# Softmax division by a diagonal product, a projection's input in quarters, and a later residual load in a hybrid attention and DeltaNet layer

## The chip, the cores and the metric

The kernel runs on one core of a Trainium2 chip. The metric is the device time of one execution in microseconds (us), taken as the median of three runs. Inside the core, TensorE (PE) multiplies matrices, VectorE (DVE), ScalarE (ACT) and GpSimd (POOL) work element by element, and the queues of SyncE (SP) and ScalarE issue transfers. TensorE has a granted clock, given in profiles as a share of 2.4 GHz; 0.50 is its lower level, 1.2 GHz.

## The reference

One layer of a decoder over 1024 positions of width 1024, all in float32. Two groups of heads read one projection of the normalized input, and their outputs are put side by side and projected back.

```
u = rmsnorm(h, norm_mix);  proj = u @ w_in          # 1024 x 2824
aq, ak, av, dq, dk, dv, dz, db, da = split(proj)
# group A: 8 query heads, 2 key heads of 64, blocks of 128 queries, each sees its own and the previous block
s = where(valid, q.k * scale, -inf)
probs = softmax(concat([s, sink]))[..., :-1];  o = probs @ v
# group B: gated DeltaNet, 4 heads of 128, chunks of 64: convolution, SiLU, an inverse per chunk, a scan over 16 chunks
h += concat([attn_out, dn_out]) @ w_o
h += square(relu(rmsnorm(h) @ w_up)) @ w_down
h += sigmoid(rmsnorm(h) @ w_ple_gate) * (p @ w_ple_proj)     # p: 1024 x 256, w_ple_proj: 256 x 1024
out = rmsnorm(h, norm_final)
```

The softmax divides each row of exponentials by its sum (with the sink in it).

## The kernel before

The positions are worked in two halves of 512 (hb = 0 and 1). Large products run in three passes: `split` (L218) writes the rounded part of a float32 tile with ACT and the remainder with POOL or DVE, and PE adds high x high, high x low and low x high. `wunit2` (L277) loads one piece of a weight (128x512) through SP, and splits it.

The order of the work is made when the program is built. Functions are written as generators. An object `flow` keeps a clock of its own: `Pe` (L93 to L107) adds an assumed duration for each product and transposition, `yield 2.5` means "not before 2.5 us from now", and at each step the first task whose time has come is asked for its next piece. If none is due, a piece of `flow.filler` is taken, which is the list of large projections in `projections` (L1085); if that is held up, a piece of `flow.spare`. A float32 product of 128 columns counts twice what a transposition counts in this clock. So a task with more assumed work lets fewer pieces of the filler in between, and they come later.

Four places matter here.

- Attention. `attention` (L585) goes through 32 units of 128 queries and two heads. `att_scores` (L532) makes the scores, the masked maximum (DVE), the exponentials and their sum (ACT), the reciprocal and the division (DVE, L558, on tile `s`). Three units later `att_pt` (L561) transposes the divided probabilities on PE, by products with the identity `con` (through L106), into a PSUM bank from the ring "d", copies them to `pt`, and `att_pv` multiplies by the values.
- `embed` (L1049) computes p @ w_ple_proj as the spare work. It loads p by halves (`pr`, L1055) and splits each half into AT0, of which there is one buffer: the second half's split waits until all products of the first half are done. For each of 4 column groups there are 4 blocks of positions, each pair of blocks a bank: 12 products, an ACT copy into `po` (two buffers, L1072), and a store to `PD` in HBM by SP (L1075).
- `w_out` (L1004) multiplies the concatenated heads by w_o and adds the residual x, which an ACT queue loads by two blocks of 1 MB at the start (L1006, into tiles H and AT).
- The scan of group B: a chain of small steps on PE, DVE and ACT per chunk (products with `St`, `vn`, `oS`), for hb = 0 beside `embed`, for hb = 1 beside `w_out`. The last scan steps of hb = 1 use oss, Z and oS.

After them come the two MLP products and the rest, which the change doesn't touch.

Of the kernel before, what the change touches and what calls it, by code (L numbers as in the profile page):

```python
# [10 lines left out]
F32 = mybir.dt.float32  # L11
F32R = mybir.dt.float32r
AF = mybir.ActivationFunctionType
ALU = mybir.AluOpType
# [4 lines left out]
P = 128  # L19
# [4 lines left out]
HB = 512  # L24
# [7 lines left out]
WN = 2 * NKV  # L32
# [77 lines left out]
def bc(ap, dim, n):  # L110

    a = ap.unsqueeze(dim)
    shape = list(a.shape)
    shape[dim] = n
    return a.to_broadcast(shape)
# [3 lines left out]
def hybrid_block(ctx, tc, t, out):  # L119
    nc = tc.nc  # L120
    V, A, G, SY = nc.vector, nc.scalar, nc.gpsimd, nc.sync
    flow = Flow()
    T = Pe(tc, flow)
    cnt = [0]

    def nm(s):
        cnt[0] += 1
        return f"{s}{cnt[0]}"
# [6 lines left out]
    wraw = pool("wraw", bufs=2)  # L135
# [39 lines left out]
    def part(tag, dt=F32):  # L175

        return keep.tile([P, 2048], dt, tag=tag, name=nm(tag))
# [6 lines left out]
    ident = con[:, K_ID:K_ID + P]  # L184
# [33 lines left out]
    def split(hi, lo, src, lo_eng):  # L218
        A.copy(hi, src)  # L219
        lo_eng.tensor_tensor(lo, src, hi.bitcast(F32), op=ALU.subtract)  # L220
# [227 lines left out]
    atp = atx.__enter__()  # L448
# [84 lines left out]
    def att_scores(n, gp, kv, qT):  # L533

        lo = 0 if n else P
        h0 = kv * 4 + gp * 2
        st = lambda x: atp.tile([P, 2], F32, tag=x, name=nm(x), bufs=4)
        b, free = yield from take("d")
        mx, sm = st("mx"), st("sm")
        s = atp.tile([P, 2, 257], F32, tag="s", name=nm("s"), bufs=4)  # L540
        G.tensor_copy(s[:, :, 256], sinkB[:, h0:h0 + 2])
        b = b.rearrange("p (g s) -> p g s", g=2)
        j = slice(n % 4 + lo // P, n % 4 + 2)
        for i in range(2):
            o = b[:, i, lo:256].rearrange("p (j s) -> p j s", s=P)
            T.matmul(o, qT[:, kv, gp * 2 + i], kH[:, kv, j], start=True, stop=False)
            T.matmul(o, qT[:, kv, gp * 2 + i], kL[:, kv, j], start=False, stop=True)
        for i in range(2):
            V.tensor_tensor_reduce(
                out=s[:, i, lo:256], in0=b[:, i, lo:256], in1=amask[:, lo:256],  # L550
                scale=1.0, scalar=NEG, op0=ALU.add, op1=ALU.max, accum_out=mx[:, i:i + 1])
        free()
        V.scalar_tensor_tensor(mx, mx, -1.0, nsink[:, h0:h0 + 2], op0=ALU.mult, op1=ALU.min)  # L553
        for i in range(2):
            A.activation(s[:, i, lo:257], s[:, i, lo:257], AF.Exp, bias=mx[:, i:i + 1],  # L555
                         accum_out=sm[:, i:i + 1])
        V.reciprocal(sm, sm)
        V.tensor_tensor(s[:, :, lo:256], s[:, :, lo:256], bc(sm, 2, 256 - lo), op=ALU.mult)  # L558
        return s

    def att_pt(n, kv, s):  # L561
        b, free = yield from take("d")
        b = b.rearrange("p (k g s) -> p k g s", k=2, g=2)
        kbs = slice(0 if n else 1, 2)
        for kb in range(kbs.start, 2):
            for i in range(2):
                T.transpose(b[:, kb, i], s[:, i, kb * P:(kb + 1) * P], ident)
        pt = atp.tile([P, 2, 2, P], F32, tag="pt", name=nm("pt"), bufs=2)
        (A.copy if kv else V.tensor_copy)(pt[:, kbs], b[:, kbs])
        free()  # L570
        return pt
# [12 lines left out]
    def attention(ns):  # L584
        units = [(n, gp, kv) for n in ns for gp in range(2) for kv in range(2)]  # L585
        qT, ss, pts, b = {}, {}, {}, None
        lag = 3
        qT[ns[0]] = yield from att_q(ns[0])
        yield 3.0
        for i in range(len(units) + lag):  # L590
            if i < len(units):
                n, gp, kv = units[i]
                ss[i] = yield from att_scores(n, gp, kv, qT[n])
                scored[n].done = gp * kv == 1
                if i + 1 < len(units) and units[i + 1][0] not in qT:
                    qT[n + 1] = yield from att_q(n + 1)
            if i >= lag:
                n, gp, kv = units[i - lag]
                pts[kv] = yield from att_pt(n, kv, ss.pop(i - lag))
                if not kv:  # L600
                    yield 2.5
                    continue
                yield 2.0
                if gp == 0:
                    b, free = yield from take("d")
                att_pv(n, gp, pts, b)
                if gp:
                    free()
                yield 1.76
            else:  # L610
                yield 1.08
# [387 lines left out]
    def hT(hb, j, n=1):  # L999

        x, o = (H, XW + j * HB) if hb == 0 else (H, j * HB) if j < 4 else (AT[1], (j - 4) * HB)
        return x[:, o:o + n * HB]

    def w_out(hb):  # L1004
        for j in (0, 4):
            A.dma_start(hT(hb, j, 4).rearrange("p (j s) -> p j s", j=4),  # L1006
                        t["xT"].rearrange("(j p) s -> p j s", p=P)[:, j:j + 4, hb * HB:hb * HB + HB])

        def rhs(b, kt):
            return dn1[b][:, kt - 4] if hb and kt > 3 else uview(R1, b, kt)  # L1010

        def steps(g, bs, ks):
            for kt in ks:
                if kt % 2 == 0:
                    w = wunit2(t["w_o"], kt // 2, g * 256, (G, G)[hb])
                for m in range(2):
                    o = kt % 2 * 256 + m * P
                    (mm3h, mm3h)[hb](bs[m][0], lambda a: w[:, a, o:o + P], lambda b: rhs(b, kt), kt == 0, kt == KT - 1)
                    if kt < KT - 1 or m == 0:
                        yield  # L1020
            if kt == KT - 1:
                for m in range(2):
                    h = hT(hb, g * 2 + m)
                    V.tensor_tensor(h, bs[m][0], h, op=ALU.add)
                    bs[m][1]()
                yield

        early = ["gg", "ge", "ee"] if hb else []
        held = []
        for g, names in enumerate(early):  # L1030
            if "e" in names:
                yield prepped
            bs = []
            for k in names:
                bs.append((yield from take(k)))
            yield from steps(g, bs, range(4))
            held.append(bs)
        if hb:
            yield pairs_done[1]
        for g in range(4):  # L1040
            if g < len(held):
                yield from steps(g, held[g], range(4, KT))
                continue
            bs = []
            for k in "gg":
                bs.append((yield from take(k)))
            yield from steps(g, bs, range(KT))

    def embed():  # L1049

        for hb in range(2):
            pT = part("AT0", F32R).rearrange("p (b k s) -> p b k s", b=2, k=2)
            for kt in range(2):
                raw = wraw.tile([P, WN], F32, tag="raw", name=nm("pr"))[:, :HB]
                SY.dma_start(raw, t["pT"][kt * P:(kt + 1) * P, hb * HB:(hb + 1) * HB])  # L1055
                split(pT[:, 0, kt], pT[:, 1, kt], raw, G)
            for g in range(4):
                w = wunit2(t["w_proj"], 0, g * 256, G)
                for m in range(0, 4, 2):
                    ring["g"].n -= 1  # L1060
                    b = bank(ps["g"])
                    for kt in range(2):
                        for i in range(2):
                            for j, (x, y) in enumerate(PASSES):
                                T.matmul(b[:, i * 256:i * 256 + 256],
                                         pT[:, x, kt, (m + i) * P:(m + i + 1) * P],
                                         w[:, y, kt * 256:kt * 256 + 256],
                                         start=kt + i + j == 0, stop=kt * i == 1 and j == 2)
                            if kt + i < 2:
                                yield  # L1070
                    o = cvp.tile([P, HB], F32, tag="cv", name=nm("po"))
                    A.copy(o, b)  # L1072
                    ring["g"].n += 1
                    r = hb * HB + m * P
                    SY.dma_start(PD[r:r + 2 * P, g * 256:g * 256 + 256].rearrange("(i p) c -> p i c", p=P),  # L1075
                                 o.rearrange("p (i c) -> p i c", i=2))
                    yield
# [52 lines left out]
    b = bank(ps["e"])  # L1130
# [351 lines left out]
    for kt in range(KT):  # L1482
        for nh in range(2):
            i = kt * 2 + nh
# [11 lines left out]
    for tt in range(NT):  # L1496
# [8 lines left out]
        for q in range(2):  # L1505
            b = bank2()
# [99 lines left out]
```

## Time and profile before

| | us |
|---|---|
| median of three runs | 1365.46 (1364.79 to 1365.91) |
| the profiled execution | 1366.2 |
| its span | 1364.1 |
| PE busy in the span | 1317.7 (97%) |
| DVE busy | 838.8 (61%) |
| ACT busy | 548.0 (40%) |
| POOL busy | 434.5 (32%) |

The profiled execution is 2.1 us longer than its span. In that execution attention runs from about 80 to 290 us, the embedding product between about 390 and 450, w_out from 445 to 565, and the MLP after 565. The rows below carry all numbers of the prediction. A row with a start shows when a run of like instructions began, how long it took until its last one ended, and in square brackets what the engine waited for ahead of it.

### The profile page before, as it was taken

To read this page: it belongs to the slowest core of one execution; us is meant where nothing else is said; L and a number is where in the kernel's file an instruction comes from. 1 tells how busy PE (TensorE), PEld (TensorE's weight loads), DVE (VectorE), ACT (ScalarE), POOL (GpSimd) and SP (SyncE) were. 2 spreads that over 40 slices of the span, in tenths; PEclk is the share of its full clock that TensorE was granted. 3 is DMA by queue.
4 is the path that set the end of the run, shared out by engine and by line. 5 is a ranking of instruction groups with operands and counts; after the bars stand their busy time and mean duration, and the time that the engine had idled before them with its cause. 6 is when DMAs were issued, how large, how long until landed. Compare 5 with 4: busy or idle time off the path is not lost.

```text
span 1364.1 us, 20392 instructions
## 1 busy us (share of the span) xinstructions
PE 1317.7 (97%) x7664; PEld 1125.5 (83%) x7664; DVE 838.8 (61%) x1558; ACT 548.0 (40%) x1083; POOL 434.5 (32%) x430
## 2 busy tenths in 40 slices
PE   8999999999998999898999999999999999999997
PEld 6788688999897998886788888877888888888886
DVE  6786977697564755797776676654333343344553
ACT  6456375544544433564333333342122231221333
POOL 6673626631385452300011111103122212210332
PEclk9999999999999999999999999999999999999999
DMA  6322222324135431321433323354333333232211
GB/s 223 88 54 73 54 62 52 74 73 105 34 119 176 133 110 33 115 85 63 146 116 116 124 87 114 109 185 136 96 116 101 98 123 120 77 93 73 75 62 47
DMA packets 102738, 134.33 MB, mean 98 GB/s; under 512 B 16400, under 2 KB 71744, under 8 KB 102384
## 3 DMA queue, kind: packets, MB, share of 16 engines
q1 hardware_dynamic: 90528, 110.50, 27.0%
q10 hardware_dynamic: 11760, 21.77, 4.4%
q8 instruction: 60, 0.98, 0.3%
q0 software_dynamic: 352, 0.76, 0.2%
q14 instruction: 38, 0.31, 0.1%
HBM read 106.77 MB, written 26.23 MB: 98 GB/s over the span
## 4 chain that ended last, share of the span: by engine, by line
PE 74%; DVE 11%; DMA 6%; ACT 3%; issue 3%; POOL 2%; SPq 1%; POOLq 0%; ACTq 0%; DVEq 0%
PE bk L102 72%; PE bk L106 2%; DVE w L220 1%; DVE cv L412 1%; DMA AD<-t 1%; ACT w L219 1%; DMA raw<-in_w_in 1%; POOL rsb L358 1%; DMA PD<-po 1%; DMA raw<-in_w_down 1%; DMA H<-in_w_in 1%; DMA AT<-in_xT 0%; DVE gg L649 0%; DMA raw<-AD 0%; SPq L841 0%
## 5 line engine op out<-in xcount | busy, mean ns | idle before, releaser
L102 PE MATMUL bk<-T,w 128*128 128x512 f32 x2304 | 537.9, 392 | 5.7 <-ACT w L219 4.5
L102 PEld LDWEIGHTS bk<-T,w 128*128 128x128 f32 x2304 | 432.8, 188 | 102.6 <-ACT w L219 6.6
L220 POOL TENSOR_TENSOR w<-raw,w 128x512 fp32r<-128x512 f32 x136 | 180.5, 1329 | 621.3 <-ACT w L219 590.2
L219 ACT CAST w<-raw 128x512 fp32r<-128x512 f32 (+1 forms) x280 | 172.6, 620 | 460.8 <-PE bk L102 340.6
L102 PE MATMUL bk<-R,w 128*128 128x256 f32 (+1 forms) x1536 | 240.7, 312 | 1.4 <-ACT w L219 1.4
L102 PEld LDWEIGHTS bk<-R,w 128*128 128x128 f32 x1536 | 210.8, 189 | 22.9 <-issue 2.3
L220 DVE TENSOR_TENSOR w<-raw,w 128x512 fp32r<-128x512 f32 (+1 forms) x144 | 107.5, 748 | 61.1 <-ACT w L219 60.9
L1478 DVE TENSOR_TENSOR H<-bk,H 128x512 f32<-128x512 f32 x96 | 64.6, 690 | 96.0 <-PE bk L102 96.0
L102 PE MATMUL bk<-U,w 128*128 128x512 f32 (+1 forms) x384 | 80.3, 355 | 1.0 <-ACT ba L472 0.6
L102 PEld LDWEIGHTS bk<-U,w 128*128 128x128 f32 x384 | 60.2, 191 | 14.5 <-issue 4.9
L102 PE MATMUL bk<-w,R 128*128 128x256 f32 (+1 forms) x480 | 69.4, 294 | 0.1
L102 PE MATMUL bk<-w,U 128*128 128x256 f32 (+2 forms) x384 | 64.1, 321 | 5.2 <-ACT AT L478 3.2
L102 PE MATMUL bk<-AT,w 128*128 128x256 f32 (+1 forms) x256 | 65.3, 342 | 1.3 <-DVE t L1363 0.8
L102 PEld LDWEIGHTS bk<-w,U 128*128 128x128 f32 x384 | 55.6, 194 | 12.3 <-ACT AT L478 3.4
L102 PEld LDWEIGHTS bk<-w,R 128*128 128x128 f32 x480 | 61.7, 192 | 4.0 <-issue 3.1
L1348 ACT ACTIVATE t<-t 128x512 f32<-128x512 f32 x64 | 40.3, 631 | 39.1 <-DVE t L1347 38.4
L102 PEld LDWEIGHTS bk<-AT,w 128*128 128x128 f32 x256 | 42.8, 191 | 8.3 <-DVE t L1363 1.9
L102 PE MATMUL bk<-R,T 128*128 128x512 f32 (+1 forms) x204 | 48.7, 386 | 0.0
L220 POOL TENSOR_TENSOR T<-ra,T 128x1024 fp32r<-128x1024 f32 x14 | 33.6, 2398 | 46.7 <-ACT T L219 41.0
L102 PE MATMUL bk<-T,T 128*128 128x512 f32 (+1 forms) x204 | 47.0, 379 | 0.0
L555 ACT ACTIVATE s<-s,mx 128x257 f32<-128x257 f32 (+1 forms) x64 | 31.3, 492 | 36.8 <-DVE mx L553 30.2
L102 PEld LDWEIGHTS bk<-T,T 128*128 128x128 f32 x204 | 36.8, 188 | 7.8
(370 smaller groups left out, 1882.1 us busy)
## 6 DMA issues: line engine op xcount, KB each, us to landing
raw<-in_w_in SPq DMA_DIRECT2D x72, 256.0 KB, 2.8
raw<-in_w_up SPq DMA_DIRECT2D x32, 512.0 KB, 4.9
AD<-t ACTq DMA_DIRECT2D x64, 256.0 KB, 2.7
raw<-in_w_down SPq DMA_DIRECT2D x64, 256.0 KB, 3.0
ra<-AD SPq DMA_DIRECT2D x28, 512.0 KB, 4.1
raw<-in_w_o SPq DMA_DIRECT2D x32, 256.0 KB, 3.1
PD<-po SPq DMA_DIRECT2D x16, 256.0 KB, 3.7
rawg<-in_w_gate SPq DMA_DIRECT2D x16, 256.0 KB, 3.2
```

The source lines that it names most:

```text
L102: self.tc.nc.tensor.matmul(o, lh, rh, **k)
L106: self.tc.nc.tensor.transpose(o, x, i)
L219: A.copy(hi, src)
L220: lo_eng.tensor_tensor(lo, src, hi.bitcast(F32), op=ALU.subtract)
L358: eng.tensor_tensor(acc, acc, xr, op=ALU.add)
L412: V.scalar_tensor_tensor(cv if i < 3 else x[:, 3:], x[:, i:i + HB], cw[:, j, i:i + 1], cv, op0=ALU.mult, op1=ALU.add)
L555: A.activation(s[:, i, lo:257], s[:, i, lo:257], AF.Exp, bias=mx[:, i:i + 1], accum_out=sm[:, i:i + 1])
L1348: A.activation(r, r, AF.Square)
L1478: V.tensor_tensor(h, bs[m], h, op=ALU.add)
```

## The change

Three edits.

1. The division of `s` by its sum is taken out. In its place DVE multiplies the identity by the reciprocal sums (`att_diag`), which makes two 128x128 diagonals, `dg`, for each unit; this is written when the scores of the unit after next begin. The transposition becomes a float32 product of `s` with `dg`, which transposes and divides.
2. `embed` loads and splits p by quarters of the positions: two in the two places of AT0, the third in a tile of its own (`pT`), the fourth in the first place again.
3. `w_out` of the second half copies 8 columns of the first half's residual, which the first output group has added to, into the place of its own, ahead of its loads, and loads the later block first. The load of the first block so stands behind that output group of the first half.

```diff
-        V.tensor_tensor(s[:, :, lo:256], s[:, :, lo:256], bc(sm, 2, 256 - lo), op=ALU.mult)
-        return s
+        return s, sm
+    def att_diag(s, sm):
+        dg = atp.tile([P, 2, P], F32, tag="dg", name=nm("dg"), bufs=2)
+        V.tensor_tensor(dg, bc(ident, 1, 2), bc(sm, 2, P), op=ALU.mult)
+        return s, dg
...
-                T.transpose(b[:, kb, i], s[:, i, kb * P:(kb + 1) * P], ident)
+                T.matmul(b[:, kb, i], s[:, i, kb * P:(kb + 1) * P], dg[:, i], start=True, stop=True)
...
+            if i - 2 in ss:
+                ss[i - 2] = att_diag(*ss[i - 2])
...
+    def x_in(hb, j):
+        A.dma_start(hT(hb, j, 4).rearrange("p (j s) -> p j s", j=4),
+                    t["xT"].rearrange("(j p) s -> p j s", p=P)[:, j:j + 4, hb * HB:hb * HB + HB])
     def w_out(hb):
-        for j in (0, 4):
-            A.dma_start(hT(hb, j, 4).rearrange("p (j s) -> p j s", j=4),
-                        t["xT"].rearrange("(j p) s -> p j s", p=P)[:, j:j + 4, hb * HB:hb * HB + HB])
+        if hb:
+            A.copy(hT(1, 0)[:, 0:8], hT(0, 1)[:, 0:8])
+        for j in (4, 0)[::1 - 2 * (hb == 0)]:
+            x_in(hb, j)
...
+        two = part("AT0", F32R).rearrange("p (i b s) -> p i b s", i=2, b=2)
+        extra = dx.tile([P, 2, HB], F32R, tag="pT", name="pT")
+        places = [two[:, 0], two[:, 1], extra, two[:, 0]]
+        def quarter(i):
+            raw = wraw.tile([P, WN], F32, tag="raw", name=nm("pr"))[:, :HB]
+            SY.dma_start(raw.rearrange("p (k s) -> p k s", k=2),
+                         t["pT"].rearrange("(k p) s -> p k s", p=P)[:, :, i * 256:i * 256 + 256])
+            split(places[i][:, 0], places[i][:, 1], raw, G)
+        quarter(0)
+        quarter(1)
         for hb in range(2):
-            pT = part("AT0", F32R).rearrange("p (b k s) -> p b k s", b=2, k=2)
-            for kt in range(2):
-                raw = wraw.tile([P, WN], F32, tag="raw", name=nm("pr"))[:, :HB]
-                SY.dma_start(raw, t["pT"][kt * P:(kt + 1) * P, hb * HB:(hb + 1) * HB])
-                split(pT[:, 0, kt], pT[:, 1, kt], raw, G)
+            if hb:
+                quarter(3)
             for g in range(4):
+                if hb == 0 and g == 2:
+                    quarter(2)
```

The order of the instructions moves with it. The first place is the embedding product on PE (operands `w` and AT or pT) beside the scan of the first half. Before, in the middle of the first half of positions:

```order
L102 MATMUL bk_5198<-w_5195,AT_4923 128x256
L102 MATMUL bk_4483<-rD_4304,mgtR 128x512 x2
L102 MATMUL bk_4393<-St_3391,H 128x128 x4
L102 MATMUL bk_5214<-w_5195,AT_4923 128x256
L102 MATMUL bk_4536<-xk_2845 128x128 x4
L102 MATMUL bk_5198<-w_5195,AT_4923 128x256 x11
L102 MATMUL bk_5214<-w_5195,AT_4923 128x256 x4
L102 MATMUL bk_4589<-xq_2846,xk_2845 128x128 x4
L102 MATMUL bk_4640<-rD_4489,mgtR 128x512
```

After the change, in the middle of the embedding product:

```order
L102 MATMUL bk_5256<-w_5232,AT_4955 128x256 x4
L102 MATMUL bk_5281<-w_5278,pT 128x256
L102 MATMUL bk_5302<-w_5278,AT_4955 128x256
L102 MATMUL bk_4836<-St_3359,xk_2939 128x128 x2
L102 MATMUL bk_4836<-St_3359,xq_2940 128x128 x2
L102 MATMUL bk_5281<-w_5278,pT 128x256 x11
L102 MATMUL bk_5302<-w_5278,AT_4955 128x256 x11
L102 MATMUL bk_5323<-w_5320,pT 128x256
L102 MATMUL bk_5339<-w_5320,AT_4955 128x256
L102 MATMUL bk_5381<-w_5378,pT 128x256
L102 MATMUL bk_5323<-w_5320,pT 128x256 x11
```

The embedding product's 192 products now stand nearly in one piece behind most of the scan of the first half, since five more pieces of w_in come ahead of it.

The second place is what POOL has to do in that piece, from the second of its weights on: splits of weights (`w`), of p (`pT`, AT) and of the scan's result (R), and the multiplication of z by a row.

```order
L220 TENSOR_TENSOR w_5118<-raw_5116,w_5118 128x512
L774 MEMSET et_4994 128x512
L951 TENSOR_TENSOR oss_4583<-oss_4583,mhalf 128x2
L778 MEMSET et_4994 64x16 x2
L437 TENSOR_TENSOR z_3364<-z_3364,rows 128x512 x4
L220 TENSOR_TENSOR pT<-pr_5168,pT 128x512
L220 TENSOR_TENSOR w_5174<-raw_5172,w_5174 128x512
L220 TENSOR_TENSOR R_75<-Z_79,R_75 128x512 x2
L951 TENSOR_TENSOR oss_4654<-oss_4654,mhalf 128x2
L220 TENSOR_TENSOR w_5232<-raw_5230,w_5232 128x512
L220 TENSOR_TENSOR AT_4955<-pr_5272,AT_4955 128x512
```

Before, POOL's splits of embedding weights stand between decay tables of the scan's preparation:

```order
L220 TENSOR_TENSOR w_5122<-raw_5120,w_5122 128x512
L724 TENSOR_TENSOR rD_4304<-con,gh_3433 128x512
L724 TENSOR_TENSOR rD_4304<-con,gl_3434 128x512
L944 TENSOR_TENSOR oss_4227<-oss_4227,mhalf 128x2
L437 TENSOR_TENSOR z_3396<-z_3396,rows 128x512 x4
L737 TENSOR_TENSOR et_4301<-et_4301,con 128x512
L220 TENSOR_TENSOR w_5195<-raw_5193,w_5195 128x512
```

The multiplications of z and the splits of the scan's result now fall among the splits that the embedding product waits for.

The third place is the end of the second half's scan on PE. Before, its last steps (`St`, `vn`, `oS`) stand by themselves:

```order
L102 MATMUL bk_6087<-vn_6062,kd_5935 128x128 x2
L102 MATMUL bk_6087<-vn_6062,ka_4652 128x128 x2
L102 MATMUL bk_6416<-AT_5500,w_6629 128x256
L102 MATMUL bk_6417<-AT_5500,w_6629 128x256
L106 MATMUL bk_5951<-con,oS_5918 128x128 x2
L102 MATMUL bk_6199<-St_3391,W_6161 128x128 x2
L102 MATMUL bk_6199<-St_3391,xq_2846 128x128 x2
L106 MATMUL bk_6087<-con,oS_6056 128x128
L102 MATMUL bk_6233<-vn_6204,ka_4805 128x128 x2
L106 MATMUL bk_6087<-con,oS_6056 128x128
L102 MATMUL bk_6347<-St_3391,W_6295 128x128 x2
L102 MATMUL bk_6347<-St_3391,xq_2846 128x128 x2
```

After the change, the same steps:

```order
L102 MATMUL bk_6374<-St_3359,W_6316 128x128 x2
L102 MATMUL bk_6374<-St_3359,xq_2940 128x128 x2
L102 MATMUL bk_6361<-R_75,w_6422 128x256 x4
L102 MATMUL bk_6449<-R_75,w_6453 128x256 x6
L102 MATMUL bk_6450<-R_75,w_6453 128x256 x6
L102 MATMUL bk_6449<-R_75,w_6453 128x256 x6
L102 MATMUL bk_6450<-R_75,w_6453 128x256 x5
L106 MATMUL bk_6259<-con,oS_6224 128x128
L102 MATMUL bk_6450<-R_75,w_6453 128x256
L106 MATMUL bk_6259<-con,oS_6224 128x128
L102 MATMUL bk_6449<-R_75,w_6482 128x256 x5
L102 MATMUL bk_6395<-vn_6379,ka_4834 128x128 x2
```

Products of w_out (`R`, `w`) now stand between the last steps.

## Rows read from the trace of the kernel before

**Rows 1.** The page: busy time of the engine (us, share of span, instructions)

```profile
PE 1317.7 (97%) x7664; PEld 1125.5 (83%) x7664; DVE 838.8 (61%) x1558; ACT 548.0 (40%) x1083; POOL 434.5 (32%) x430
```

**Rows 2.** The page: shares of the chain that ended last, by engine

```profile
PE 74%; DVE 11%; DMA 6%; ACT 3%; issue 3%; POOL 2%; SPq 1%; POOLq 0%; ACTq 0%; DVEq 0%
```

**Rows 3.** Windows: length, busy us per engine (instructions), granted clock, DMA share, GB/s

```profile
80.00:290.00 210.00, 203.26 (x1454) 177.10 (x1453) 167.24 (x419) 118.96 (x280) 109.53 (x142) 0.98 0.24 61
...
390.00:450.00 60.00, 51.19 (x383) 49.61 (x382) 33.36 (x74) 28.80 (x69) 38.82 (x38) 0.89 0.58 180
450.00:500.00 50.00, 50.00 (x480) 49.19 (x479) 31.54 (x81) 18.39 (x34) 29.53 (x24) 1.00 0.40 115
500.00:565.00 65.00, 58.47 (x540) 54.77 (x539) 36.90 (x106) 26.75 (x83) 16.71 (x18) 0.97 0.17 50
```

**Rows 4.** Windows of low granted clock, same columns

```profile
154.40:157.60 3.20, 3.20 (x8) 2.48 (x8) 3.20 (x9) 1.86 (x4) 2.71 (x3) 0.50 0.17 17
...
441.10:447.80 6.70, 4.43 (x20) 4.43 (x21) 3.20 (x6) 3.49 (x9) 3.21 (x3) 0.50 0.63 180
553.70:557.00 3.30, 2.84 (x14) 2.44 (x13) 1.42 (x6) 1.12 (x5) 0.70 (x1) 0.50 0.00 0
```

**Rows 5.** Waits of PE in 80:290: us, times, longest

```profile
PE bk L106 <- DVE s L558: 3.0, 1, 3.0
PE bk L106 <- DVE gg L652: 2.6, 1, 2.6
```

**Rows 6.** Waits of PE in 390:450

```profile
PE bk L102 <- ACT po L1072: 3.8, 1, 3.8
```

**Rows 7.** Waits of PE in 500:565

```profile
PE bk L106 <- DVE oS L949: 2.3, 2, 1.2
PE bk L102 <- DVE kvs L858: 1.9, 2, 1.4
```

**Rows 8.** Timeline of PE, 218:223: start, us to the last end, instructions

```profile
218.48 0.60 PE L106 MATMUL bk<-con,AT 128*128 128x128 f32 x4
218.92 0.60 PE L106 MATMUL bk<-con,s 128*128 128x128 f32 x4
219.28 0.36 PE L102 MATMUL bk<-w,U 128*128 128x256 f32 x1
220.84 1.16 PE L102 MATMUL bk<-H 128*128 128x128 f32 x8 [1.21 <-DVE ka L751]
221.76 1.43 PE L102 MATMUL bk<-w,U 128*128 128x256 f32 x10
```

**Rows 9.** Lines by form: busy us, mean ns, idle before

```profile
L106 PE MATMUL bk<-con,s 128*128 128x128 f32 x120 | 19.4, 275 | 5.5 <-DVE s L558 3.0 <-DVE gg L652 2.6
L558 DVE TENSOR_TENSOR s<-s,sm 128x512 f32<-128x512 f32 x28 | 26.0, 928 | 0.6
L558 DVE TENSOR_TENSOR s<-s,sm 128x256 f32<-128x256 f32 x4 | 2.5, 617 | 0.0
```

**Rows 10.** Timeline of DVE ahead of the stall at 152.81

```profile
145.28 3.55 DVE L649 SCALAR_TENSOR_TENSOR gg<-gg,sf 128x16 f32<-128x16 f32 x5
...
149.58 1.30 DVE L558 TENSOR_TENSOR s<-s,sm 128x512 f32<-128x512 f32 x1
```

**Rows 11.** The chain of waits in 404:452: start, us, what

```profile
432.57 10.09 DMA PD<-po
```

**Rows 12.** DMA issues in 430:446: count, size, median us to landing

```profile
H<-in_xT ACTq DMA_DIRECT2D x2, 1024.0 KB, 9.4
PD<-po SPq DMA_DIRECT2D x4, 256.0 KB, 7.0
```

**Rows 13.** DMA issues in 389:430

```profile
PD<-po SPq DMA_DIRECT2D x9, 256.0 KB, 2.2
```

**Rows 14.** Timeline of PE in the embedding product

```profile
396.70 3.09 PE L102 MATMUL bk<-w,AT 128*128 128x256 f32 x24
399.63 0.61 PE L102 MATMUL bk<-vn,kd 128*128 128x128 f32 x4
```

**Rows 15.** Lines of POOL in 390:450

```profile
L220 POOL TENSOR_TENSOR w<-raw,w 128x512 fp32r<-128x512 f32 x10 | 12.9, 1296 | 7.4 <-ACT w L219 6.8 <-POOL et L771 0.5
...
L437 POOL TENSOR_TENSOR z<-z,rows 128x512 f32<-128x512 f32 x4 | 5.1, 1309 | 0.0
L944 POOL TENSOR_TENSOR oss<-oss,mhalf 128x2 f32<-128x2 f32 x5 | 3.5, 697 | 2.9 <-DVE oss L943 2.1 <-ACT po L1072 0.8
...
L724 POOL TENSOR_TENSOR rD<-con,gh 128x512 fp32r<-128x512 f32 x3 | 3.1, 1044 | 4.2 <-PE bk L102 4.2
```

More of the change, by code (lines that the diff above doesn't have):

```diff
@@ L557, in att_scores, with att_pt @@
         V.reciprocal(sm, sm)
-        V.tensor_tensor(s[:, :, lo:256], s[:, :, lo:256], bc(sm, 2, 256 - lo), op=ALU.mult)
-        return s
-    def att_pt(n, kv, s):
+        return s, sm
[3 more added lines that the diff above has]
+        return s, dg
+    def att_pt(n, kv, s, dg):
         b, free = yield from take("d")
@@ L598, in attention @@
                 n, gp, kv = units[i - lag]
-                pts[kv] = yield from att_pt(n, kv, ss.pop(i - lag))
+                pts[kv] = yield from att_pt(n, kv, *ss.pop(i - lag))
                 if not kv:
@@ L1049, in embed @@
     def embed():
-        for hb in range(2):
-            pT = part("AT0", F32R).rearrange("p (b k s) -> p b k s", b=2, k=2)
-            for kt in range(2):
-                raw = wraw.tile([P, WN], F32, tag="raw", name=nm("pr"))[:, :HB]
-                SY.dma_start(raw, t["pT"][kt * P:(kt + 1) * P, hb * HB:(hb + 1) * HB])
-                split(pT[:, 0, kt], pT[:, 1, kt], raw, G)
+        two = part("AT0", F32R).rearrange("p (i b s) -> p i b s", i=2, b=2)
[8 more added lines that the diff above has]
+        quarter(1)
+        for hb in range(2):
+            if hb:
+                quarter(3)
             for g in range(4):
+                if hb == 0 and g == 2:
+                    quarter(2)
                 w = wunit2(t["w_proj"], 0, g * 256, G)
                 for m in range(0, 4, 2):
+                    pT = places[hb * 2 + m // 2]
                     ring["g"].n -= 1
@@ L1065, in embed @@
                                 T.matmul(b[:, i * 256:i * 256 + 256],
-                                         pT[:, x, kt, (m + i) * P:(m + i + 1) * P],
+                                         pT[:, x, kt * 256 + i * P:kt * 256 + i * P + P],
                                          w[:, y, kt * 256:kt * 256 + 256],
```

## Prediction

> **What bounds the kernel now.** I read the page's busy times first: TensorE is busy for 97% of the span [rows 1]. Then the chain of waits: three quarters of it is TensorE itself, the rest small steps on DVE, transfers and ACT [rows 2]. So the time is TensorE's work plus a few places where it stands still, and a change is worth the work it adds or takes from TensorE and the stalls it makes or removes there. Third, the windows show the three places that the change reaches [rows 3]. In attention (80 to 290 us) TensorE is busy for 203.26 of 210 us. In the embedding product (390 to 450) it is busy for 51.19 of 60, and the granted clock is 0.89. In the last stretch of w_out (500 to 565) it is busy for 58.47 of 65 at 0.97. Between the last two lies a stretch of w_out beside the scan with 50.00 of 50 busy: where the filler has enough independent products, the scan's waits cost nothing.
>
> Stalls cost twice here. The granted clock stands at 0.50, the lower level of 1.2 GHz, for about 3.3 us at 154.4, for 6.7 us at 441.1 and for 3.3 us at 553.7 [rows 4], each time just behind a wait of TensorE: 2.6 us on gg, 3.8 us on po, and several of about 1 us on oS [rows 5, 6, 7]. At half speed 3.3 us hold 1.65 us of full-speed work, so such a dip costs 1.65 us, and it goes with its stall. A single wait of 1.21 us at 220.84 [rows 8] has no dip of that kind among the rows shown.
>
> **The change part by part.**
>
> *TensorE's work in attention, +13.8 us.* There are 120 transpositions of s [rows 9]. Four transpositions of AT take from 218.48 to 218.92, 0.44 us, which is 0.11 each; the four of s behind them take 0.36, 0.09 each. The float32 products of the trace show what replaces them: the products of H with itself stand as eight records for four 128x128 products, from 220.84 to 221.76, 0.92 us, so 0.115 per record and 0.23 per product [rows 8]. Each transposition becomes such a product, that is, one more record of 0.115 us: 120 x 0.115 = 13.8 us. The ends are 120 x (0.23 - 0.11) = 14.4 and, with the cheapest transposition, 120 x (0.23 - 0.09) = 16.8 above; below, 120 x 0.09 = 10.8 if only a transposition's own price is added. I take 13.8, by the shorter arithmetic from the record itself. Nothing hides it, since TensorE is the bound here.
>
> The Trainium skill, page "FP8 and Floating Point Precision", section "TensorE Precision Notes", says that true float32 takes four passes through the array. The rows show two records per product and 0.23 us. By four passes at a transposition's 0.11 the product would cost 0.44 and the change 120 x 0.33 = 40 us. The measurement decides, and I keep two.
>
> *DVE in attention.* It loses 28 divisions of 128x512 at 0.93 us and 4 of 128x256 at 0.62 [rows 9], 28.5 us in all, and gains 32 products of 128x256. By the 128x256 division's mean these take 32 x 0.62 = 19.8 us, so DVE gets 8.7 us back, 0.3 per unit, while TensorE's work per unit grows by 4 x 0.115 = 0.46. DVE thus gains some 0.7 us on TensorE per unit. Also, the diagonal is made one unit or more ahead of its use. Two stalls stand in this stretch, 3.0 us on s at the first unit and 2.6 on gg [rows 5]. The first stays: the first unit's diagonal needs the same exponentials and reciprocal. The second is DVE being late: five tiny gg steps take 3.55 us there and a division 1.30 behind them [rows 10]. The lead of about ten units at 0.7 us covers 2.6, and so the stall goes with its dip: -2.6 - 1.65 = -4.2 us. Bounds: 0 if it stays, -4.2 if it goes. I take -4.2.
>
> *The embedding product, -5.3 us.* The stretch 390 to 450 loses 8.8 us of TensorE idle time and (1 - 0.89) x 60 = 6.6 us by the clock [rows 3], 15.4 in all. Its largest wait is 3.8 us on po [rows 6], and the chain shows why: a store of po to PD took 10.09 us [rows 11], when two residual loads of 1 MB, 9.4 us each, ran beside it; the four stores took 7.0 us in the median there, against 2.2 before [rows 12, 13]. In the changed order the copy of 8 columns holds one of these loads back until w_out's first group is done, and the p quarters take away the wait of the second half's split on all products of the first half. So the 3.8 us with the dip of 6.7 us behind it, 3.35, mostly go. Against it: the product now runs nearly in one piece, 192 products at 2.93 / 24 = 0.122 us [rows 14], 23.4 us, with hardly any scan work between, and POOL must follow. By the changed order, from the split of the last but one w_in piece to the last split for the embedding product, POOL has 29 steps of 128x512 at 1.30, 4 decay steps at 1.04 and 4 oss steps at 0.70 [rows 15]: 37.7 + 4.2 + 2.8 = 44.7 us. TensorE has 240 products of 128x256 at 0.122, 46 small ones at 0.11 and two larger in the same stretch, 35 us. So POOL ends some 10 us later than TensorE could, unless it had a lead, and it has been idle for a third of the stretch before. I take half of that, 5, with two to three dips, 5: a loss of 10 where it was 15.3, so -5.3. Bounds: a loss of 0 (-15.4) if POOL's lead covers all, and 25 (+9.6) if the whole product ran at half clock, 23.4 more for 192 products and some.
>
> *The tail of the scan, -8.2 us.* In 500 to 565 TensorE idles for 65 - 58.47 = 6.5 us [rows 3], on oS and kvs and the like [rows 7], with one dip of 1.65. In the changed order these last scan steps have 6 to 24 products of w_out between them, as in the stretch that is 50 of 50 busy. So 6.5 + 1.65 = 8.2 go. The residual load that is held back still has the length of w_out in front of it, so it isn't late. Bounds: 0 and -8.2.
>
> Everything from the MLP on has the same order. The sum: 13.8 - 4.2 - 5.3 - 8.2 = -3.9. From the profiled 1366.2 that makes 1362.3; the median of the runs is 0.7 lower, 1365.46 - 3.9 = 1361.6 us.
>
> **The rivals.**
>
> *The second stall of attention stays* (1365.8). The 2.6 us are then not DVE's load but the tiny gg steps, which the change leaves as they are, or the new diagonal product held beside POOL's work. For it: 3.55 us for five 128x16 steps, and 1.30 for a division whose mean is 0.93 [rows 9, 10]. Against it: the steps are spread otherwise in the changed order. Sum: -3.9 + 4.2 = +0.3.
>
> The Trainium skill, page "SBUF — State Buffer", section "SBUF: two separate sides", says that DVE and GpSimd hold a shared port pair in turn, each for a whole instruction, when the DVE step has two SBUF inputs. The stretched 1.30 agrees with it, and the diagonal product has two SBUF inputs as well; by that rule it could be held for one POOL step, about 1.3 us, each time.
>
> *POOL starves the embedding product* (1371.6, slower). Place: the 192 products behind the scan. Mechanism: each split that comes late idles TensorE, and the granted clock stays at 0.50 in such a stretch, as at 441.1, where TensorE was busy for 4.43 of 6.70 us and slow besides [rows 4]. For it: the 44.7 against 35 us, and the z multiplications, R splits and weight splits that stand in front of each other. Against it: POOL was only 38.82 of 60 us busy in the same place [rows 3]. Price: the loss is between 16 (10 of idle time and 6.6 of clock, as now) and 25; at 20 it is +4.7 in place of -5.3: 13.8 - 4.2 - 8.2 + 4.7 = +6.1. It decides from a loss of 16.6 on, where the sum is above +2.7.
>
> *The tail isn't filled* (1369.8). The scan's chain runs later on DVE and ACT than the order has it, so that TensorE waits at the same steps, only with w_out's products behind them. For it: the chain's steps have the same lengths. Against it: the full stretch at 450. Sum: -3.9 + 8.2 = +4.3.
>
> *The embedding product loses nothing* (1351.5). POOL's idle third before it gives a lead of 10 us. Sum: 13.8 - 4.2 - 15.4 - 8.2 = -14.0.
>
> **How the numbers follow.** A difference under 0.2%, 2.7 us, can't be told from no change; faster is below 1362.7, slower above 1368.2. The forecast's case, with its own range of 1358 to 1366, has 0.48: 0.36 of it faster, 0.10 the same, 0.02 slower. The stall that stays has 0.16, all the same. The starved product has 0.20 and the unfilled tail 0.08, both slower. The better case has 0.08, faster. So faster 0.44, the same 0.26, slower 0.30. The range of 1355 to 1372 leaves out most of the better case and the upper part of the starved one.
>
> **What the changed profile would show.** The product of s with dg as 240 records of about 0.115 us, and TensorE's busy time in attention up by 14; no wait on gg or on a scores bank near 155; no wait on po over 2 us, and no store to PD of 10 us; waits on weight splits of POOL in the embedding product, under 6 us in sum; no oS or kvs waits in w_out's last 60 us. A product record of 0.2 us, a clock of 0.5 through the embedding product, or oS waits as before would make the prediction wrong.

## The result, and the profile after

The changed kernel takes 1375.93 us in the median of 6 runs (1373.89 to 1380.75), against 1365.87 for the kernel before in the same series: 1.0082 times as long, with a 95% interval from 1.0067 to 1.0097 (the ratio is estimated over all runs; the two medians alone give 1.0074). The forecast was 1361.6 us in a range up to 1372; the time went the other way, by 10.1 us. The profiled execution after has a span of 1374.0 us, 9.9 more than before.

The stretches of the new profile come first, as in [rows 3]: length, busy us of PE, PEld, DVE, ACT and POOL, granted clock, DMA share, GB/s. The stretches follow the new places: attention, the first inverse of the DeltaNet part, the embedding product, the start of w_out, and its end.

```profile
80.00:296.00 216.00, 212.31 (x1531) 185.38 (x1531) 159.12 (x423) 119.08 (x277) 106.45 (x140) 0.99 0.23 57
316.00:336.00 20.00, 17.21 (x157) 16.56 (x155) 13.03 (x24) 5.66 (x9) 2.27 (x2) 0.83 0.33 84
...
425.00:466.00 41.00, 31.81 (x242) 30.03 (x241) 27.72 (x86) 21.54 (x45) 25.69 (x23) 0.96 0.62 188
466.00:500.00 34.00, 31.20 (x351) 29.67 (x350) 10.29 (x26) 10.40 (x23) 14.94 (x13) 1.00 0.48 146
500.00:565.00 65.00, 64.38 (x579) 62.77 (x579) 39.75 (x100) 30.08 (x88) 28.68 (x27) 1.00 0.24 74
```

Attention idles for 3.7 us instead of 6.7. The last row is the tail: 0.6 us idle at full clock, where [rows 3] had 6.5 at 0.97. The embedding product idles for 9.2 us in 41. The second and fourth row are places that had no term in the forecast: 2.8 us idle and a granted clock of 0.83 at the first inverse, 2.8 us idle at the start of w_out.

The products that replaced the transpositions, and the diagonals (busy us, mean ns, idle before), answer to [rows 9]:

```profile
L102 PE MATMUL bk<-dg,s 128*128 128x128 f32 x240 | 33.8, 278 | 2.9 <-DVE dg L563 2.9
L563 DVE TENSOR_TENSOR dg<-con,sm 128x256 f32<-128x256 f32 x32 | 16.9, 527 | 0.0
```

There are 240 records and 14.4 us more of PE busy time than the transpositions' 19.4. DVE spends 16.9 us in place of 28.5. The wait on gg is gone; the one of 2.9 us at the first unit stays.

**The wait at the first inverse.** PE's timeline shows two waits just after SP's queue carried the inverse's store (XD) and its eight loads (Xt):

```profile
321.71 0.68 PE L102 MATMUL bk<-XT,ka 64*64 64x64 f32 x16 [0.65 <-issue]
...
328.60 1.12 PE L102 MATMUL bk<-XT,ka 64*64 64x64 f32 x16 [2.14 <-ACT ex L670]
```

SP's queue in the same stretch:

```profile
312.29 2.14 SPq L281 DMA_DIRECT2D raw<-in_w_in  x2
314.48 1.11 SPq L791 DMA_DIRECT2D XD<-et  x2
318.01 3.67 SPq L848 DMA_DIRECT2D Xt<-XD  x8
321.78 8.39 SPq L281 DMA_DIRECT2D raw<-in_w_in  x4
```

And ScalarE, which casts the weights:

```profile
317.00 0.62 ACT L219 CAST w<-raw 128x512 fp32r<-128x512 f32 x1 [1.35 <-DMA raw<-in_w_in]
325.78 0.62 ACT L219 CAST w<-raw 128x512 fp32r<-128x512 f32 x1 [8.16 <-DMA raw<-in_w_in]
...
327.04 1.28 ACT L670 ACT_TABLE_LOAD   x1
```

From 314.48 to 321.78 SP issues no weight load: it waits for the store to land, then issues eight loads. ScalarE waits 8.16 us for the next weight, the table load and `ex` stand behind that cast, and PE stands behind `ex`.

The kernel before has the same store and loads in SP's queue, but one weight load stands between them, and PE has products of w_in up to the inverse's first step:

```profile
319.45 1.11 SPq L784 DMA_DIRECT2D XD<-et  x2
320.70 0.50 SPq L281 DMA_DIRECT2D raw<-in_w_in  x1
322.43 4.52 SPq L841 DMA_DIRECT2D Xt<-XD  x8
```

And PE before:

```profile
314.75 14.19 PE L102 MATMUL bk<-R,w 128*128 128x256 f32 x118
328.87 0.68 PE L102 MATMUL bk<-XT,ka 64*64 64x64 f32 x16
```

There this place cost 0.7 us of waiting. So the queue was held up before too; what is new is that PE has less work ready. Of the 80 loads of w_in, SP had issued 72 ahead of the store before, and 66 after. The granted clock after the two waits is 0.50 for 6.8 us:

```profile
328.00:334.80 6.80, 6.21 (x40) 6.09 (x41) 6.03 (x12) 2.28 (x5) 0.62 (x1) 0.50 0.38 88
```

Idle time 2.8 and 3.4 for the clock make 6.2 us.

**The waits in the embedding product.** PE's waits between 425 and 466 us (us, times, longest) answer to [rows 6]:

```profile
PE bk L102 <- DVE St L941: 4.1, 1, 4.1
PE bk L102 <- ACT po L1098: 1.8, 2, 1.4
PE bk L102 <- ACT w L219: 1.5, 2, 1.2
PE bk L106 <- DVE oS L956: 1.1, 1, 1.1
PE bk L102 <- POOL w L220: 0.5, 1, 0.5
```

The largest is a scan step on DVE. DVE's timeline shows why it was late: a step of the next half's preparation stood ahead of it in DVE's queue and waited 5.72 us for a transfer (rD from LD).

```profile
434.91 1.95 DVE L782 TENSOR_TENSOR rD<-rD,bS 128x1024 f32<-128x1024 f32 x1 [5.72 <-DMA rD<-LD]
436.79 0.41 DVE L868 TENSOR_TENSOR kd<-bk,ex 128x256 f32<-128x256 f32 x1
437.12 0.59 DVE L941 SCALAR_TENSOR_TENSOR St<-St,ex,bk 128x128 f32<-128x128 f32 x2
```

The chain of waits ahead of it shows that this transfer, too, reads back what SP's queue has just stored:

```profile
423.67 6.50 DMA LD<-ka
...
430.72 4.07 DMA rD<-LD
```

The store took 6.50 us to land, where the stores to LD take 1.5 in the median; DVE, and PE behind it, waited for both.

**The second inverse.** The chain of waits ahead of PE's wait of 2.77 us on XT is again a store and its loads:

```profile
471.01 3.97 DMA XD<-et
...
476.37 2.08 DMA Xt<-XD
478.58 0.46 DVE XT L809
479.08 3.00 PE bk L102 x34
```

### The profile page after: what moved, and what is told of

Its sections match the earlier page's. It is cut to its first block, busy times and chain, and to the rows that moved or that the text cites. A ratio compares the mean times of both kernels' runs of the same rounds, so it can differ in the third digit from the quotient of the medians.

```text
span 1374.0 us, 20645 instructions
## 1 busy us (share of the span) xinstructions
PE 1330.4 (97%) x7784; PEld 1137.6 (83%) x7784; DVE 837.3 (61%) x1558; ACT 552.6 (40%) x1085; POOL 441.0 (32%) x430
## 4 chain that ended last, share of the span: by engine, by line
PE 75%; DVE 8%; DMA 8%; ACT 3%; POOL 3%; issue 2%; SPq 1%; POOLq 0%; DVEq 0%; ACTq 0%
PE bk L102 73%; PE bk L106 2%; DMA AD<-t 1%; DMA raw<-in_w_in 1%; DVE w L220 1%; ACT w L219 1%; POOL w L220 1%; DMA raw<-in_w_down 1%; POOL rsb L358 1%; DMA H<-in_w_in 1%; DMA raw<-in_w_up 1%; DMA raw<-in_w_proj 1%; DMA XD<-et 1%; DMA AT<-in_xT 0%; DMA LD<-ka 0%
## 5 line engine op out<-in xcount | busy, mean ns | idle before, releaser
L220 POOL TENSOR_TENSOR w<-raw,w 128x512 fp32r<-128x512 f32 x136 | 184.8, 1362 | 584.2 <-ACT w L219 578.5
L102 PE MATMUL bk<-R,w 128*128 128x256 f32 (+1 forms) x1536 | 250.1, 317 | 1.8 <-ACT w L219 1.8
L102 PEld LDWEIGHTS bk<-R,w 128*128 128x128 f32 x1536 | 215.5, 191 | 24.6 <-issue 3.5
L102 PEld LDWEIGHTS bk<-U,w 128*128 128x128 f32 x384 | 59.5, 188 | 14.4 <-issue 4.7
```

The costliest lines, as they stand in the source:

```text
L102: self.tc.nc.tensor.matmul(o, lh, rh, **k)
```

## The experiments

Theory W: the second record of each product is the loss, 13.8 us of PE work. Theory S: a good part of the loss comes from the order, because the plan counts a product with the diagonal as longer than a transposition, and so other work lands elsewhere. Ratios are to runs of the kernel before in the same series. Differences between runs of different series are between medians; the series' own medians of the kernel before lie between 1365.87 and 1367.49 us, so such a difference is good to about 2 us. In the code, `[...]` stands for an index. The parts come first.

### The softmax part alone

This run has the first of the three edits alone, as shown in the change: the division becomes `att_diag`, the transposition a product with `dg`.

> Only the softmax part of the change; embed and w_out as before. Theory A (the second record of each of the 120 products, 13.8 us of TensorE work, is the loss, and only the second stall of attention, 4.2 us, comes back): 1365.9 + 13.8 - 4.2 = 1375.5 us, no different from the whole change within 2 us. Theory B (the loss comes from the quarters and from the held-back residual load, and the softmax part alone pays for itself through the filled tail): 1362 to 1366 us.

Measured: 1385.01 us against 1367.49, ratio 1.0128 (1.0106 to 1.0150). That is more than either theory expected, and more than the whole change. Its profile shows PE's waits between 425 and 475 us:

```profile
PE bk L102 <- ACT w L219: 7.4, 2, 6.9
PE bk L102 <- ACT po L1079: 2.9, 3, 1.7
PE bk L102 <- POOL w L220: 2.4, 1, 2.4
```

The chain of waits ahead of the 6.9 us:

```profile
452.33 0.33 POOL R L220
452.66 0.89 issue
453.55 2.50 POOL AT L220 x2
456.05 0.02 issue
456.07 3.21 DMA raw<-in_w_proj
459.28 0.02 issue
459.31 0.63 ACT w L219
```

POOL splits the second half of p (AT) only behind splits of the scan's result (R), and the next weight's load stands behind that. This is the rival of the starved embedding product, in the kernel without the quarters. The wait at the first inverse is there too (0.6 and 2.2 us).

### The quarters alone

This run has the second edit alone, as shown in the change.

> Only p in quarters. Theory A: the embedding product loses about 3 us less than before, 1362 to 1364 us. Theory B (the quarters cost more than they give): 1368 us or more.

Measured: 1363.33 us, ratio 0.9961 (0.9945 to 0.9977), faster than both kernels. The embedding stretch is at full clock and 6.9 us idle, where [rows 3] had 8.8 at 0.89:

```profile
390.00:450.00 60.00, 53.14 (x439) 51.25 (x438) 31.79 (x73) 30.18 (x69) 41.29 (x40) 1.00 0.63 192
```

PE waits for po for 1.9 us in two pieces there instead of 3.8 at once, with the residual loads as before.

### The held-back residual alone, and with the quarters

```diff
+        if hb:
+            A.copy(hT(1, 0)[:, 0:8], hT(0, 1)[:, 0:8])
+        for j in (4, 0)[::1 - 2 * (hb == 0)]:
+            x_in(hb, j)
```

> Only the held-back residual load. Theory A: the store of po to PD that took 10 us is short and the wait of 3.8 us on po with its dip of 3.4 us goes: 1359 to 1362 us. Theory B (the load is late for w_out of the second half, or another wait takes the place): 1366 us or more.

Measured: 1370.55 us, ratio 1.0021 (1.0006 to 1.0035). Theory A of this run fell: the po waits of 2.1 and 1.0 us still stand in its profile, and a wait of 2.2 on XT is new.

> Quarters and held-back residual without the softmax part, so transpositions and the division as before. Theory A: faster than before by 5 to 9 us, 1357 to 1361 us, and 15 us faster than the whole change. Theory B: 1366 us or more.

Measured: 1365.19 us, ratio 0.9987 (0.9973 to 1.0000), neither of the two ranges for sure. The held-back load takes something from the quarters' gain: the intervals of the two ratios overlap by 0.0004 only.

### The plan's share

In these four the instructions stay and only the number that the plan adds for one of them is changed: products with the diagonal are planned as transpositions, or transpositions as products. This doesn't bring the other kernel's order back: with the shorter plan SP issues 69 loads of w_in ahead of the first inverse's store, where the kernel before issues 72 and the softmax part with its real length 66.

```diff
 T.matmul(b[:, kb, i], s[...], dg[:, i], start=True, stop=True)
+flow.now += 0.11 - 4 * P / 2400      # softmax part, planned as transpositions
...
 T.transpose(b[:, kb, i], s[...], ident)
+flow.now += 4 * P / 2400 - 0.11      # transpositions, planned as products
```

> Only the softmax part, but the order is planned as if a product with the diagonal took no longer than a transposition (0.11 us), so more of w_in stays ahead of the first inverse. Theory W (the loss is the 14 us of TensorE work): no different from the softmax part planned by its real length, 1382 to 1388 us. Theory S (a good part of the loss comes from the order that the longer plan makes, with bare steps at the first inverse and a starved second half of p): faster than it by 6 us or more, 1379 us or less.

Measured: 1371.30 us, ratio 1.0043 (1.0028 to 1.0058). It is 13.7 us faster than the softmax part with its real length in the plan (0.85% by the ratios), with the same products on PE. Here theory S holds. Its tail is full, as the profile's last window of w_out shows:

```profile
500.00:565.00 65.00, 65.00 (x587) 63.36 (x586) 35.43 (x94) 29.77 (x82) 28.64 (x26) 1.00 0.24 75
```

> The kernel before, with nothing changed but that the plan takes each of the 120 transpositions as long as a product with the diagonal (0.213 us). Theory S (the order that a longer plan makes costs time by itself): slower than before by 5 to 9 us, as it was beside the quarters and the held-back load. Rival (that cost belongs to the combination with the quarters): within 2 us of before.

Measured: 1372.32 us, ratio 1.0050 (1.0035 to 1.0065). No product and no transfer is added, and 6 us are lost. Its waits between 400 and 450 us are many small ones of the scan and of weights, the longest 1.4 us:

```profile
PE bk L102 <- ACT w L219: 2.6, 2, 1.4
PE bk L102 <- ACT oS L914: 2.0, 2, 1.3
PE bk L102 <- ACT vn L920: 1.6, 3, 0.7
```

But waits aren't what it lost. Up to the first product of the MLP its window is

```profile
80.00:592.81 512.81, 490.93 (x3920) 447.59 (x3918) 361.65 (x858) 255.60 (x576) 243.14 (x254) 0.97 0.30 83
```

TensorE is idle there for 21.9 us, against 23.0 before, and busy for 9.9 us more, at a granted clock of 0.97 against 0.98. The wait at the first inverse isn't in it either; 72 loads of w_in stand ahead of the store, as before. So this loss isn't the one of the whole change.

> Quarters and held-back residual; transpositions and division as before, but each transposition planned as long as a product with the diagonal (0.213 us). Theory W: no different from the same without the plan's change, 1362 to 1368 us. Theory S: slower than that by 4 us or more, 1369 us or above.

Measured: 1372.93 us, ratio 1.0048 (1.0030 to 1.0065), 7.7 us above the same parts without the plan's edit. Theory S again.

> The whole change, with a product with the diagonal planned as long as a transposition. Theory W: as the whole change, 1374 to 1378 us. Theory S: the 6.2 us at the first inverse go, 1366 to 1371 us.

Measured: 1374.54 us, ratio 1.0066 (1.0044 to 1.0089), not to be told from the whole change. Here S fell: in its profile PE doesn't wait at the first inverse, but waits of 2.5 us each on w and XT and of 2.1 on oS, and 1.8 on H, stand elsewhere. The wait at the first inverse is missing in all three kernels with the softmax part and the shorter plan, and present in the whole change, in the softmax part alone and in softmax part and quarters with the real length. So the plan's number makes that wait, but taking it out gave the whole change nothing that is clear of the noise.

### The price of a product

```diff
+nc.tensor.matmul(b[:, kb, i], s[...], dg[:, i], start=True, stop=True)
 T.matmul(b[:, kb, i], s[...], dg[:, i], start=True, stop=True)
```

> The whole change with each of the 120 products with the diagonal done twice, 240 records of 0.11 us more, the second overwriting the first. Theory W (TensorE has no slack in attention, each record costs its full length): 1376 + 26 = 1402 us, 1398 or more. Rival (part of it lies in waits that would be there anyway): 1376 + 13 = 1389 us or less.

Measured: 1403.41 us, ratio 1.0283 (1.0240 to 1.0326), 27.5 us above the whole change: 27.5 / 240 = 0.115 us per record. The second record isn't counted in the plan, so this run changes the work and not the plan. That the quotient comes out so well is partly chance. Up to the first product of the MLP the profile shows

```profile
80.00:616.10 536.10, 521.24 (x4290) 480.76 (x4290) 359.24 (x867) 261.42 (x585) 237.47 (x255) 0.99 0.28 79
```

The MLP starts 21.9 us later than in the whole change, with TensorE busy for 26.9 us more and idle for 5.0 less. The other 6 us of the profiled execution lie in the MLP, in waits of 3.6 and 3.0 us that the whole change doesn't have; why they are there wasn't looked into. The busy time gives 26.9 / 240 = 0.112 us per record, so the forecast's price of a record was right. Attention itself idles for 3.0 us in this run and 3.7 in the whole change, so it has hardly any slack.

### Softmax part and quarters, without the held-back load

> The whole change without the held-back residual load. If that load costs about 3 us, as it did alone: 1371 to 1374 us. If it costs nothing beside the other two parts: 1375 to 1378 us.

Measured: 1378.08 us, ratio 1.0085 (1.0058 to 1.0111). No cost of the held-back load beside the other two parts can be told from the noise.

> Softmax part and quarters, a product with the diagonal planned as long as a transposition. If the quarters give 4 us and the old plan's order is as good as in the softmax part alone: 1371 - 4 = 1367 us. If the gain of quarters and of plan is the same wait: 1371 us or more.

Measured: 1377.60 us, ratio 1.0081 (1.0055 to 1.0107), 6 us slower than the softmax part alone with this plan. So the quarters give 4 us alone and 7 beside the softmax part, and cost 6 beside the softmax part in the other plan (5, 6 and 5 by the ratios): such gains don't add up.

### The queue at the first inverse

```diff
-            SY.dma_start(s["XD"][...], XS[...])
+            (A if s is s01[0] else SY).dma_start(s["XD"][...], XS[...])
...
-            SY.dma_start(X[...], xd[tt, blk])
+            (A if s is s01[0] and tt < 2 else SY).dma_start(X[...], xd[tt, blk])
```

> The whole change, with the store of the first inverse (XD) and its eight loads (Xt) issued by ScalarE's queue in place of SP's, so that weight loads on SP no longer stand behind them. Theory Q (the wait at 326 us and the low clock behind it come from SP standing still from 314.5 to 321.8 us): these 5.5 us go, 1369 to 1372 us. Rival (the inverse itself is late, whatever the queue): 1374 to 1378 us, the wait at the first XT stays.

Measured: 1372.19 us, ratio 1.0042 (1.0028 to 1.0056), 3.7 us below the whole change; the intervals of the two ratios don't meet. PE's timeline has no wait at the inverse any more:

```profile
315.83 8.00 PE L102 MATMUL bk<-R,w 128*128 128x256 f32 x66
323.75 0.68 PE L102 MATMUL bk<-XT,ka 64*64 64x64 f32 x16
...
325.06 4.04 PE L102 MATMUL bk<-R,w 128*128 128x256 f32 x32
```

And SP issues weight loads through the whole stretch:

```profile
308.38 22.60 SPq L281 DMA_DIRECT2D raw<-in_w_in  x8
```

Theory Q holds for this wait. It gives 3.7 of the 6.2 us back: the order moves once more with the edit, and a wait of 3.6 us on a POOL split appears in the embedding product.

## Why the prediction was wrong

**The work, +13.8 us: right for the products themselves, too small for the whole.** 240 records, 14.4 us more busy time, and 0.112 us of busy time per record when they are doubled. But TensorE's other products got longer, by about 4 us in sum; the account is below. The prediction's side sum of 40 us took a transposition's 0.11 us for one pass. The kernel's own plan counts 4 x 128 / 2400 = 0.213 us for such a product, close to the 0.23 that the rows show; so they speak against that price of a pass, and not against the four passes that the prediction cites.

**DVE in attention, -4.2 us: right.** The wait on gg and the low clock behind it are gone. Both kernels with transpositions and the longer plan still have the wait (2.5 and 2.3 us), so it went with the softmax part and not with the plan.

**The tail, -8.2 us: right in its place.** 0.6 us idle remain of 6.5, at full clock. In the other runs, the 65 us that end 19 us ahead of the first MLP product have at most 0.9 us idle in every kernel with the softmax part, and 3 to 6 in every kernel with transpositions; the quarters and the held-back load don't fill them.

**The embedding product, -5.3 us: about right in size, by luck.** The stretch loses 9.2 us idle and (1 - 0.96) x 41 = 1.6 by the clock, 10.8, where the forecast had 10. The loss is less POOL than foreseen (0.5 us of waiting for its splits, 1.5 for ACT's casts); the largest wait is a scan step behind a DVE step that waits for a store to HBM and its load back. The wait on po shrank, but the held-back load was not the reason: alone it leaves 3.1 us of po waits, while the quarters alone cut them to 1.9, and both together leave 3.8.

**The failed step is the sum.** It took out the stalls that the new order fills, and held no term for waits that the new order makes outside the three stretches it looked at. Six loads of w_in moved behind the first inverse's store, and so PE has less work ready while SP's queue carries the inverse's store and loads. That wait costs 6.2 us with its low clock, and the second inverse 2.8; both come from a store to HBM and the loads of it in SP's queue. Only the first was tested by a run; the second is read from the trace. With them the account up to the MLP is 13.8 - 4.2 - 0.4 (a shorter wait in attention) + 5.5 (6.2 less 0.7 at the first inverse before) - 3.8 (the embedding product and the 0.8 us of waits just ahead of it) + 2.8 - 7.6 = +6.1, where the MLP starts 10.2 us later. The stalls so gave back 7.7 us, where the prediction had 17.7; that is 10 of the 14 us by which the sum missed.

Of the four rivals, two would have made the kernel slower: the tail unfilled, which didn't come, and the embedding product starved, which is what the softmax part alone does, since p is still in halves there; the quarters take 7 us of it away. The signs that the prediction listed were nearly all seen (no wait on gg, 1.8 us on po in two waits, no store to PD over 4.0 us, 0.5 us on POOL's weight splits, a single oS wait of 0.6 us in the tail), but all of them lie in the three stretches.

**The other 4 us are work.** TensorE's windows from 80 us to the first MLP product, before and after:

```profile
80.00:584.04 504.04, 481.05 (x3921) 441.88 (x3920) 356.45 (x860) 251.33 (x574) 237.98 (x254) 0.98 0.30 84
80.00:594.22 514.22, 494.35 (x4042) 454.28 (x4042) 358.80 (x865) 257.42 (x579) 243.11 (x254) 0.99 0.30 83
```

TensorE is idle for 3.1 us less and busy for 13.3 us more, although fewer microseconds at half clock lie in it: 20.9 us of the busy time before (from 89.5, 154.3, 406.9, 420.6, 441.0 and 553.7 us) and 12.4 after (from 89.2, 328.1 and 437.3). At full speed its work thus grew by 13.3 + (20.9 - 12.4) / 2 = 17.6 us, where the prediction had 13.8. The stalls gave back 3.1 of idle time and 4.3 by the clock, 7.4, and 17.6 - 7.4 is the 10.2.

An estimate from the traces, with each record counted up to the start of the next and time at half clock halved, gives 487.7 to 488.8 us of such work in the kernels with the softmax part, whichever the plan (the doubled products aside), and 470.5 to 475.3 in those with transpositions. So most of the added work goes with the softmax part, and not with the plan's number.

**What stays open.** By the same estimate the products with the diagonal take 13.9 us more than the transpositions, as forecast, and the 1152 products of R with w take 126 ns each instead of 123, which is 4.3 us; what makes them longer wasn't found. It is also open where the 6 to 8 us come from that the longer plan costs beside transpositions, and why the quarters cost 6 us beside the softmax part under the shorter plan.

## What to carry to other kernels

Work added to an engine that is 97% busy added its full length to the busy time here, and what it gives back must be shown stall by stall. Add up the engine's idle time, its time at half clock and its work at full speed for the whole stretch too: that shows what no listed wait holds. Where a plan sets the order, a change of an assumed duration is a change of its own: time it alone and beside the part that brings it. Here it cost 6 us alone and 14 beside the softmax part, and beside the whole change no difference could be told. And follow each store that is read back through the same queue: what stands behind it in the new order is the next candidate for a wait.

## What was not expected of the hardware

A queue that carries a store and the loads of what was stored issued nothing else for 7.3 us (314.48 to 321.78), and the engine at the end of the line, TensorE, lost 2.8 us to waiting and 3.4 to the clock, which stood at 0.50 for 6.8 us behind waits of 0.65 and 2.14 us. The single wait of 4.14 us at 433.5 had 0.50 behind it only from 437.3 to 440.5, and the one of 2.77 us at 476.3 had none (the window of 466 to 500 stands at 1.00), so the length of a wait didn't tell the length of the low clock.
